# Attention scores of a hybrid decoder layer as half-array products, with keys and transposes laid out for it

## The chip, the cores and the metric

One core of one Trainium2 chip runs the whole layer as one program. The metric is the device time of one execution in microseconds (us). Before the change the median of three runs is 2406.98 us (2406.73 to 2409.63).

## The reference, cut to what matters

One decoder layer over 2048 tokens of width 1024, all in 32-bit floats. After a modulated RMS norm, one input projection feeds two parallel groups of heads: sliding-window attention (8 query heads of 64, 2 key/value heads, window 128, a learned sink per head) and a state-space scan. Both go through one output projection; then come a second norm, a SwiGLU feed-forward part and a last norm. The change touches the attention alone:

```python
def sliding_window_attention(q, k, v, sinks):
    ...
    kb, vb = band(k), band(v)          # the token block before and the block itself
    scores = jnp.einsum('bnqhgd,bnkhd->bnhgqk', qb, kb).astype(jnp.float32)
    scores = scores * (1.0 / math.sqrt(HEAD_DIM))
    ...
    mask = (diff >= 0) & (diff < WINDOW) & (kpos[:, None, :] >= 0)
    scores = jnp.where(mask[None, :, None, None], scores, -jnp.inf)
    ...
    m = jnp.maximum(jnp.max(scores, axis=-1, keepdims=True), sink)
    p = jnp.exp(scores - m)
    denom = jnp.sum(p, axis=-1, keepdims=True) + jnp.exp(sink - m)
    probs = (p / denom).astype(v.dtype)
    out = jnp.einsum('bnhgqk,bnkhd->bnqhgd', probs, vb)
```

The sum over d, the 64 elements of a head, is the product that the change rebuilds: q has heads g = 0 to 3 for each key group h = 0 and 1.

## The kernel before

The tokens are cut into 4 blocks of 512 (b = 0 to 3), each into 4 token tiles of 128 (t). Every operand of a large product is split into a high part that TensorE takes as it is and a low part that holds the rest (`split`, `halves`: a copy on ACT, a subtraction on DVE or POOL), and a product is three matmuls: high by high, high by low, low by high (`mm3`, lines 272 to 275). A matmul names its stationary operand first (the weights that PEld loads), then the moving one; its name in the profile is out<-moving,stationary.

The program runs a main stream of dense products on TensorE (queries, keys and values, convolution inputs, gates, output projection, then the feed-forward part as `quads` and `down`) and puts *side steps* between its chunks: `attentions(b)` and `ssds(b)` are generators, each `yield` ends one side step, and `beside` takes on average 1.1 (MIX), 0.5 or 0.64 side steps after each chunk of the main stream. `both` takes a step of the one and a step of the other in turn. A chunk is mostly twelve dense matmuls.

TensorE's instructions follow the order in which the code issues them up to the end of `gated(3)` (a manual schedule); later ones, and those of DVE, ACT, POOL and the DMA queue, are placed by a scheduler that works with estimated times. Each engine then runs its own instructions in order.

TensorE's results lie in eight banks of 128 partitions by 512 floats: four for the dense products (d), and one each for am, at, sm and st. A bank with one buffer can't be written anew before its last reader is done. Attention has am and at, the scan has sm and st.

For each token tile, `attentions` goes through these steps:
- It turns the keys (one 128x128 transpose into am, line 549) and the queries (four into at, line 557). Partitions 0 to 63 of the turned keys belong to key group 0, partitions 64 to 127 to group 1. `k_ring` holds them for two tiles, high and low, with each group in a 128-row operand whose other 64 rows are zero (lines 551 to 554), so that one matmul over 128 rows gives both groups side by side: 128 queries by 256 columns. Queries are split by lines 560 and 561.
- For j = 0 to 3 (query head j of both groups), `scores` makes two times three matmuls of 256 columns into am (one `mm3` for the tile before, one for the tile itself), and two reductions on DVE (line 609) add the mask, store the scores and keep the maximum.
- After j = 3, `probabilities` does eight exponentials with their sums and eight scalings on ACT (lines 620 and 626).
- The tile before is held back by one round: its `transposed` (four 128x128 transposes into at, line 632, with a copy on ACT and a subtraction on DVE, lines 635 and 636) runs ahead of each `scores`, and after every second one `values` makes twelve matmuls with v_ring into am, which line 646 copies out.

Of the kernel before, what the change touches and what calls it, by code (L numbers as in the profile page):

```python
# [42 lines left out]
def hymba_layer(ctx, tc, xT, crow, pos, wada, wadk, vecs, rows, wq, wkv, wz, wx, wo, wgu, wd4, wd2, outT):  # L43
# [18 lines left out]
    def bank(tag, bufs):  # L62
        return pp.tile([P, T], F32, name=tag, tag=tag, bufs=bufs)
# [36 lines left out]
    def const(shape, name, dt=F32, pool=sb):  # L100
        return pool.tile(shape, dt, name=name, tag=name, bufs=1)
# [27 lines left out]
    amask = const([P, 2 * P], "amask")  # L129
    nc.gpsimd.memset(amask, 0.0)  # L130
    nc.gpsimd.affine_select(out=amask[:, 0:P], in_=amask[:, 0:P], pattern=[[1, P]], compare_op=ALU.is_ge,
                            fill=NEG, base=-1, channel_multiplier=-1)
# [338 lines left out]
    k_ring = const([P, 2, 2, 2, P], "k_ring", F32R)  # L471
    v_ring = const([P, 4 * 192 + 64], "v_ring", F32R)
    nc.gpsimd.memset(k_ring.bitcast(F32), 0.0)
# [40 lines left out]
    def attentions(b, m):  # L514
        late = []

        def values_of(sms, slots, t):
            got = {}

            def turn(j):  # L520
                if j % 2 == 0:
                    got["pT"] = [m.m4().rearrange("p h t -> p (h t)").rearrange("p (b j k) -> p b j k", b=4, j=2)
                                 for _ in range(2)]
                transposed(sms[j], got["pT"], len(slots), j % 2)

# [7 lines left out]
            return turn, sums  # L533
# [10 lines left out]
        for t in range(NT):  # L544
            gt, (q, kv) = b * NT + t, nxt
            slot = gt % 2
            slots = [slot] if gt == 0 else [1 - slot, slot]
            ps = bank("am", 1)
            nc.tensor.transpose(ps[:, 0:P], kv[:, 0:P], ident)
            for r in range(2):  # L550
                rs = slice(r * 64, (r + 1) * 64)
                nc.scalar.copy(k_ring[rs, 0, slot, r, :], ps[rs, 0:P])
                nc.vector.tensor_tensor(k_ring[rs, 1, slot, r, :], ps[rs, 0:P],
                                        k_ring[rs, 0, slot, r, :].bitcast(F32), ALU.subtract)
# [41 lines left out]
    def scores(m, st, qhi, qlo, slots, j):  # L596
        mx = st[:, 0, :]
        ns = len(slots)
        mask = amask[:, (2 - ns) * P:].rearrange("p (s k) -> p s k", k=P)
        sc = bank("am", 1)[:, :2 * P * ns]  # L600
        js = slice(j * P, (j + 1) * P)
        for i, slot in enumerate(slots):
            mm3(sc[:, 2 * P * i:2 * P * (i + 1)], qhi[:, js], qlo[:, js],
                *(k_ring[:, h, slot].rearrange("p r k -> p (r k)") for h in range(2)), True, True)
        sc = sc.rearrange("p (s r k) -> p s r k", r=2, k=P)
        sm = m.m2().rearrange("p (r s k) -> p r s k", r=2, k=P)
        for r in range(2):
            i = 2 * j + r
            nc.vector.tensor_tensor_reduce(sm[:, r, 0:ns, :], sc[:, :, r, :], mask, 1.0, sinks[:, i:i + 1],
                                           ALU.add, ALU.max, mx[:, i:i + 1])  # L610
        return sm
# [784 lines left out]
```

## Time and profile before

| what | us |
|---|---|
| median of the three runs | 2406.98 |
| the profiled execution | 2408.73 |
| its span, first to last instruction | 2407.0 |
| PE busy (TensorE, matmul) | 2267.8 |
| DVE busy | 1445.4 |
| POOL busy | 1230.1 |
| ACT busy | 966.2 |

The mean clock granted to TensorE was 0.971. PE is TensorE's matmul stream, PEld its weight loads, which run beside it; DVE, ACT and POOL are VectorE, ScalarE and GpSimd. A record's start is real; the end of a matmul is modelled, so the time that one holds the stream is read from start to start. In a row of the timeline the first number is the start, the second the duration, and in brackets stands how long the engine had been idle before and what ended it. A row such as "PE am L273 <- DVE k_ring L553: 9.6, 6, 3.8" says that PE, at line 273 into am, waited for DVE's line 553 for 9.6 us in total, 6 times, 3.8 at the longest.

### The profile page before, as it was taken

To read this page: it belongs to the slowest core of one execution; us is meant where nothing else is said; L and a number is where in the kernel's file an instruction comes from. 1 tells how busy PE (TensorE), PEld (TensorE's weight loads), DVE (VectorE), ACT (ScalarE), POOL (GpSimd) and SP (SyncE) were. 2 spreads that over 40 slices of the span, in tenths; PEclk is the share of its full clock that TensorE was granted. 3 is DMA by queue.
4 is the path that set the end of the run, shared out by engine and by line. 5 is a ranking of instruction groups with operands and counts; after the bars stand their busy time and mean duration, and the time that the engine had idled before them with its cause. 6 is when DMAs were issued, how large, how long until landed. Compare 5 with 4: busy or idle time off the path is not lost.

```text
span 2407.0 us, 33175 instructions
## 1 busy us (share of the span) xinstructions
PE 2267.8 (94%) x11304; PEld 1887.6 (78%) x11304; DVE 1445.4 (60%) x2543; ACT 966.2 (40%) x2011; POOL 1230.1 (51%) x1227
## 2 busy tenths in 40 slices
PE   6896999999999899999999999989999999999998
PEld 4786889798879688887887788766788888878787
DVE  6877875664455865566664363499555444544544
ACT  2464552654345545533333232244333333333332
POOL 0866433453113755578785232446766666643441
PEclk9897999999999899999999999999999999999998
DMA  6798977777875422232334665574422222263441
GB/s 242 271 367 286 309 245 252 235 249 241 281 243 173 135 85 66 84 110 89 96 101 153 230 221 165 189 264 154 142 88 79 80 83 79 79 227 101 142 160 53
DMA packets 249065, 412.22 MB, mean 171 GB/s; under 512 B 22464, under 2 KB 68544, under 8 KB 248896
## 3 DMA queue, kind: packets, MB, share of 16 engines
q1 hardware_dynamic: 247744, 409.05, 51.5%
q8 instruction: 89, 1.46, 0.3%
q10 hardware_dynamic: 1152, 1.05, 0.1%
q14 instruction: 80, 0.66, 0.1%
HBM read 315.58 MB, written 94.44 MB: 170 GB/s over the span
## 4 chain that ended last, share of the span: by engine, by line
PE 67%; DVE 12%; DMA 7%; POOL 5%; issue 5%; ACT 3%; SPq 1%; DVEq 0%; POOLq 0%; ACTq 0%
PE d L273 9%; PE d L275 9%; PE d L274 9%; PE d L881 7%; PE d L880 7%; PE d L882 7%; DMA t<-in_xT_dram 2%; PE am L273 1%; PE am L274 1%; PE am L275 1%; PE am L880 1%; DMA t<-act 1%; PE am L882 1%; PE am L881 1%; DMA t<-mid 1%
## 5 line engine op out<-in xcount | busy, mean ns | idle before, releaser
L880 PE MATMUL d<-b,w 128*128 128x512 f32 x924 | 366.2, 400 | 12.0 <-ACT b L841 9.2
L881 PE MATMUL d<-b,w 128*128 128x512 f32 x924 | 368.4, 399 | 0.9 <-POOL b L842 0.9
L882 PE MATMUL d<-b,w 128*128 128x512 f32 x924 | 366.8, 398 | 0.7 <-DVE w L812 0.7
L811 ACT ACTIVATE w<-raw 128x512 fp32r<-128x512 f32 x316 | 197.5, 629 | 415.9 <-PE d L275 212.6
L273 PE MATMUL d<-a,w 128*128 128x512 f32 (+1 forms) x720 | 281.1, 398 | 22.8 <-ACT a L961 12.2
L275 PE MATMUL d<-a,w 128*128 128x512 f32 (+1 forms) x720 | 283.2, 393 | 0.0
L274 PE MATMUL d<-a,w 128*128 128x512 f32 (+1 forms) x720 | 281.9, 392 | 0.1
L812 DVE TENSOR_TENSOR w<-raw,w 128x512 fp32r<-128x512 f32 x228 | 213.1, 937 | 72.8 <-ACT w L811 72.1
L812 POOL TENSOR_TENSOR w<-raw,w 128x512 fp32r<-128x512 f32 x88 | 119.9, 1363 | 247.3 <-ACT w L811 228.4
L972 DVE SCALAR_TENSOR_TENSOR x<-d,mod,x 128x512 f32<-128x512 f32 (+1 forms) x182 | 130.7, 724 | 162.5 <-PE d L275 159.8
L880 PEld LDWEIGHTS d<-b,w 128*128 128x128 f32 x924 | 174.7, 189 | 53.5 <-ACT b L841 11.8
L273 PE MATMUL d<-w,hl 128*128 128x256 f32 (+1 forms) x608 | 181.4, 299 | 27.4 <-ACT hl L324 12.7
L881 PEld LDWEIGHTS d<-b,w 128*128 128x128 f32 x924 | 175.2, 190 | 39.9 <-POOL b L842 1.9
L882 PEld LDWEIGHTS d<-b,w 128*128 128x128 f32 x924 | 174.5, 189 | 39.8 <-DVE w L812 1.4
L812 POOL TENSOR_TENSOR w<-s,w 128x512 fp32r<-128x512 f32 x132 | 188.2, 1428 | 30.6 <-ACT w L811 29.6
L811 ACT ACTIVATE w<-s 128x512 fp32r<-128x512 f32 x176 | 110.8, 633 | 200.3 <-PE d L882 156.7
L273 PEld LDWEIGHTS d<-a,w 128*128 128x128 f32 x720 | 137.0, 191 | 60.6 <-ACT a L961 15.1
L275 PE MATMUL d<-w,hl 128*128 128x256 f32 (+1 forms) x608 | 177.7, 292 | 2.4 <-DVE hl L325 2.4
L274 PE MATMUL d<-w,hl 128*128 128x256 f32 (+1 forms) x608 | 177.2, 292 | 0.0
L274 PEld LDWEIGHTS d<-a,w 128*128 128x128 f32 x720 | 137.1, 190 | 31.6 <-DVE a L806 0.9
L896 POOL TENSOR_TENSOR s<-raw,s 128x512 f32<-128x512 f32 x44 | 59.3, 1349 | 199.1 <-DVE w L812 124.4
L275 PEld LDWEIGHTS d<-a,w 128*128 128x128 f32 x720 | 136.7, 190 | 30.8 <-issue 0.2
(356 smaller groups left out, 5486.9 us busy)
## 6 DMA issues: line engine op xcount, KB each, us to landing
raw<-in_wgu_dram SPq DMA_DIRECT2D x176, 256.0 KB, 2.7
raw<-in_wd_dram SPq DMA_DIRECT2D x176, 256.0 KB, 2.7
w<-w_x SPq DMA_DIRECT2D x48, 512.0 KB, 5.3
w<-w_o SPq DMA_DIRECT2D x48, 512.0 KB, 4.7
act<-t SPq DMA_DIRECT2D x88, 256.0 KB, 2.1
t<-act SPq DMA_DIRECT2D x88, 256.0 KB, 4.4
t<-in_xT_dram SPq DMA_DIRECT2D x80, 256.0 KB, 4.4
aw<-in_wada_dram SPq DMA_DIRECT2D x64, 256.0 KB, 4.5
```

The source lines that it names most:

```text
L273: nc.tensor.matmul(out, ahi, bhi, start=first, stop=False)
L274: nc.tensor.matmul(out, ahi, blo, start=False, stop=False)
L275: mm3.last = nc.tensor.matmul(out, alo, bhi, start=False, stop=last)
L811: nc.scalar.activation(hi, x, AF.Copy)
L812: eng.tensor_tensor(lo, x, hi.bitcast(F32), ALU.subtract)
L880: nc.tensor.matmul(out, ahi, bhi, start=first and k == 0, stop=False, skip_group_check=True)
L881: nc.tensor.matmul(out, ahi, blo, start=False, stop=False, skip_group_check=True)
L882: mm3.last = nc.tensor.matmul(out, alo, bhi, start=False, stop=k == 3, skip_group_check=True)
L896: nc.gpsimd.tensor_tensor(s4, a12, s2, ALU.subtract)
L972: nc.vector.scalar_tensor_tensor(x, ps, gate2[:, c:c + 1], x, ALU.mult, ALU.add)
```

## The change

- The keys are kept without zeros: `k_ring` is half as large, and one cast and one subtraction of 128 partitions replace two of each over 64.
- The scores of two query heads (`pair_of`) are made in one go: for each, three products by two halves r. A half takes partitions 64r to 64r + 63 of queries and keys, 64 rows of the array, and 256 columns (both tiles at once); group 0 goes to bank am and group 1 to bank at, alternating. That is twelve matmuls, then four reductions.
- The ring's slots stay in place, so the mask has a third part, and is taken rotated where the tile itself lies in slot 0.
- Transposes come in pairs: four into am, four into at, and `values` is the step after them. Scores of a pair, transposes of a pair and values of a half are side steps of their own. `probabilities` comes in the step of the second pair of scores, ahead of the transposes of the second pair.

```diff
-    amask = const([P, 2 * P], "amask")
+    amask = const([P, 3 * P], "amask")
...
-    k_ring = const([P, 2, 2, 2, P], "k_ring", F32R)
+    k_ring = const([P, 2, 2, P], "k_ring", F32R)
     v_ring = const([P, 4 * 192 + 64], "v_ring", F32R)
-    nc.gpsimd.memset(k_ring.bitcast(F32), 0.0)
...
         def values_of(sms, slots, t):
             got = {}
 
-            def turn(j):
-                if j % 2 == 0:
-                    got["pT"] = [m.m4().rearrange("p h t -> p (h t)").rearrange("p (b j k) -> p b j k", b=4, j=2)
-                                 for _ in range(2)]
-                transposed(sms[j], got["pT"], len(slots), j % 2)
-
-            def sums(half):
+            def turn(half):
+                pT = [m.m4().rearrange("p h t -> p (h t)").rearrange("p (b j k) -> p b j k", b=4, j=2)
+                      for _ in range(2)]
+                for j in range(2):
+                    transposed(sms[2 * half + j], pT, len(slots), j)
+                yield
                 if half == 0:
                     got["out"] = m.m2()
-                values(got["out"], got["pT"], slots, half)
+                values(got["out"], pT, slots, half)
                 if half:
                     nc.sync.dma_start(spill[b][0:4, :, t * P:(t + 1) * P].rearrange("c p t -> p c t"),
                                       got["out"].rearrange("p (c t) -> p c t", c=4))
-            return turn, sums
+                yield
+            return turn
 
         def load(t):
             q, kv = m.m2(), m.m1()
...
         for t in range(NT):
             gt, (q, kv) = b * NT + t, nxt
             slot = gt % 2
-            slots = [slot] if gt == 0 else [1 - slot, slot]
+            slots = [0] if gt == 0 else [0, 1]
+            mask = amask[:, P:2 * P] if gt == 0 else amask[:, (1 - slot) * P:(3 - slot) * P]
             ps = bank("am", 1)
             nc.tensor.transpose(ps[:, 0:P], kv[:, 0:P], ident)
-            for r in range(2):
-                rs = slice(r * 64, (r + 1) * 64)
-                nc.scalar.copy(k_ring[rs, 0, slot, r, :], ps[rs, 0:P])
-                nc.vector.tensor_tensor(k_ring[rs, 1, slot, r, :], ps[rs, 0:P],
-                                        k_ring[rs, 0, slot, r, :].bitcast(F32), ALU.subtract)
+            nc.scalar.copy(k_ring[:, 0, slot, :], ps[:, 0:P])
+            nc.vector.tensor_tensor(k_ring[:, 1, slot, :], ps[:, 0:P], k_ring[:, 0, slot, :].bitcast(F32), ALU.subtract)
             ps = bank("at", 1)
             for j in range(4):
                 nc.tensor.transpose(ps[:, j * P:(j + 1) * P], q[:, j * P:(j + 1) * P], ident)
...
             st = small([P, 4, 8], "ast", 1)
             yield
             sms = []
-            for j in range(4):
+            for pair_of in range(2):
+                sms.extend(scores(m, st, qhi, qlo, slots, mask, pair_of))
+                if pair_of:
+                    probabilities(st, sms, slots)
+                    if t + 1 < NT:
+                        nxt = load(t + 1)
+                yield
                 if held:
-                    held[0](j)
-                sms.append(scores(m, st, qhi, qlo, slots, j))
-                if j == 3:
-                    probabilities(st, sms, slots)
-                if j == 2 and t + 1 < NT:
-                    nxt = load(t + 1)
-                yield
-                if held and j % 2:
-                    held[1](j // 2)
-                    if j == 1:
-                        yield
+                    yield from held(pair_of)
             load_values(kv, slot)
-            if held:
-                yield
             held = values_of(sms, slots, t)
-        for j in range(4):
-            held[0](j)
-            yield
-            if j % 2:
-                held[1](j // 2)
-                yield
+        for half in range(2):
+            yield from held(half)
 
     def load_values(kv, slot):
         v = kv[:, P:2 * P].rearrange("p (r d) -> p r d", d=64)
...
-    def scores(m, st, qhi, qlo, slots, j):
+    def scores(m, st, qhi, qlo, slots, mask, pair_of):
+
         mx = st[:, 0, :]
         ns = len(slots)
-        mask = amask[:, (2 - ns) * P:].rearrange("p (s k) -> p s k", k=P)
-        sc = bank("am", 1)[:, :2 * P * ns]
-        js = slice(j * P, (j + 1) * P)
-        for i, slot in enumerate(slots):
-            mm3(sc[:, 2 * P * i:2 * P * (i + 1)], qhi[:, js], qlo[:, js],
-                *(k_ring[:, h, slot].rearrange("p r k -> p (r k)") for h in range(2)), True, True)
-        sc = sc.rearrange("p (s r k) -> p s r k", r=2, k=P)
-        sm = m.m2().rearrange("p (r s k) -> p r s k", r=2, k=P)
-        for r in range(2):
-            i = 2 * j + r
-            nc.vector.tensor_tensor_reduce(sm[:, r, 0:ns, :], sc[:, :, r, :], mask, 1.0, sinks[:, i:i + 1],
-                                           ALU.add, ALU.max, mx[:, i:i + 1])
-        return sm
+        mask = mask.rearrange("p (s k) -> p s k", k=P)
+        banks = [bank("am", 1), bank("at", 1)]
+        for e in range(2):
+            js = slice((2 * pair_of + e) * P, (2 * pair_of + e + 1) * P)
+            for n, (q, h) in enumerate(((qhi, 0), (qhi, 1), (qlo, 0))):
+                for r in range(2):
+                    rs = slice(r * 64, (r + 1) * 64)
+                    nc.tensor.matmul(banks[r][:, 2 * e * P:(2 * e + ns) * P], q[rs, js],
+                                     k_ring[rs, h, 0:ns, :].rearrange("p s k -> p (s k)"), start=e == 0 and n == 0,
+                                     stop=e == 1 and n == 2, skip_group_check=True)
+        sms = []
+        for e in range(2):
+            sm = m.m2().rearrange("p (r s k) -> p r s k", r=2, k=P)
+            for r in range(2):
+                i = 2 * (2 * pair_of + e) + r
+                sc = banks[r][:, 2 * e * P:(2 * e + ns) * P].rearrange("p (s k) -> p s k", k=P)
+                nc.vector.tensor_tensor_reduce(sm[:, r, 0:ns, :], sc, mask, 1.0, sinks[:, i:i + 1],
+                                               ALU.add, ALU.max, mx[:, i:i + 1])
+            sms.append(sm)
+        return sms
...
     def transposed(sm, pT, ns, at):
-        ps = bank("at", 1)
+        ps = bank(("am", "at")[at], 1)
         for s in range(ns):
             for r in range(2):
                 nc.tensor.transpose(ps[:, (2 * s + r) * P:(2 * s + r + 1) * P], sm[:, r, s, :], ident)
```

In what order the engines now run this is shown at three places; a row is line, operation, out<-in and size, x4 four alike in a row.

PE at a group of scores. Before, in block 0 (t = 2), after four transposes:

```order
L275 MATMUL d<-w,hl_1485 128x264
L632 MATMUL at<-ident,m_1765 128x128 x4
L273 MATMUL am<-k_ring,m_2378 128x256
L274 MATMUL am<-k_ring,m_2378 128x256
L275 MATMUL am<-k_ring,m_2378 128x256
L273 MATMUL am<-k_ring,m_2378 128x256
L274 MATMUL am<-k_ring,m_2378 128x256
L275 MATMUL am<-k_ring,m_2378 128x256
L273 MATMUL d<-w,hl_1492 128x264
```

After, in the same tile:

```order
L275 MATMUL d<-w,hl_1526 128x256
L276 MATMUL d<-w,hl_1526 128x256
L595 MATMUL am<-k_ring,m_2198 128x256
L595 MATMUL at<-k_ring,m_2198 128x256
L595 MATMUL am<-k_ring,m_2198 128x256
L595 MATMUL at<-k_ring,m_2198 128x256
```

The alternation of am and at goes on to twelve products. Before, six products of the full array follow the transposes; now twelve of half the array lie between dense products, and the transposes are elsewhere.

PE at the end of block 1, where the last tile's probabilities are turned and multiplied by the values. Before:

```order
L275 MATMUL d<-w,hl_5759 128x256
L632 MATMUL at<-ident,m_6633 128x128 x4
L273 MATMUL d<-w,hl_5766 128x256
L274 MATMUL d<-w,hl_5766 128x256
L275 MATMUL d<-w,hl_5766 128x256
```

After:

```order
L276 MATMUL d<-hl_5766,w 128x512
L628 MATMUL am<-ident,m_6371 128x128 x4
L628 MATMUL at<-ident,m_6374 128x128 x4
L274 MATMUL am<-m_6709,v_ring 128x256
L275 MATMUL am<-m_6710,v_ring 128x256
L276 MATMUL am<-m_6709,v_ring 128x256
```

Before, dense products follow the transposes, and the value products come 24 dense matmuls later; now they stand right behind the pair of transposes.

ACT at the probabilities of a tile in block 1. Before:

```order
L635 ACTIVATE m_5213<-at 128x4x128
L444 COPY cin<-d 128x512
L447 ACTIVATE s<-cin,vec 128x512
L448 ACTIVATE s<-cin,vec 128x512
L635 ACTIVATE m_5213<-at 128x4x128
L452 ACTIVATE s<-s 128x512
L620 ACTIVATE m_5029,ast<-m_5029,ast 128x256 x2
L620 ACTIVATE m_5108,ast<-m_5108,ast 128x256 x2
L620 ACTIVATE m_5229,ast<-m_5229,ast 128x256 x2
L620 ACTIVATE m_5300,ast<-m_5300,ast 128x256 x2
L621 ACTIVATE ast<-ast 128x8
```

After:

```order
L616 ACTIVATE m_5361,ast<-m_5361,ast 128x256 x2
L616 ACTIVATE m_5364,ast<-m_5364,ast 128x256 x2
L616 ACTIVATE m_5684,ast<-m_5684,ast 128x256 x2
L616 ACTIVATE m_5687,ast<-m_5687,ast 128x256 x2
L617 ACTIVATE ast<-ast 128x8
L252 ACTIVATE hl_5756<-t 128x512
L631 ACTIVATE m_5802<-am 128x4x128
L631 ACTIVATE m_5802<-at 128x4x128
```

Before, the copies of the held tile's transposes (line 635) stand ahead of the exponentials (line 620); now the copies of the second pair (line 631) stand behind them (line 616).

More of the change, by code (lines that the diff above doesn't have):

```diff
@@ L128, in hymba_layer @@
     later = later_r.bitcast(F32)
-    amask = const([P, 2 * P], "amask")
+    amask = const([P, 3 * P], "amask")
     nc.gpsimd.memset(amask, 0.0)
-    nc.gpsimd.affine_select(out=amask[:, 0:P], in_=amask[:, 0:P], pattern=[[1, P]], compare_op=ALU.is_ge,
-                            fill=NEG, base=-1, channel_multiplier=-1)
+    for before in (amask[:, 0:P], amask[:, 2 * P:3 * P]):
+        nc.gpsimd.affine_select(out=before, in_=before, pattern=[[1, P]], compare_op=ALU.is_ge, fill=NEG, base=-1,
+                                channel_multiplier=-1)
     nc.gpsimd.affine_select(out=amask[:, P:2 * P], in_=amask[:, P:2 * P], pattern=[[-1, P]],
```

## The prediction

> **What bounds the kernel now.** I read the page first, then stretches of the span, then the score products themselves. On the page I look at TensorE's busy time (PE) and at the chain that ended last.
>
> ```profile
> span 2407.0 us, 33175 instructions
> PE 2267.8 (94%) x11304; PEld 1887.6 (78%) x11304; DVE 1445.4 (60%) x2543; ACT 966.2 (40%) x2011; POOL 1230.1 (51%) x1227
> PE 67%; DVE 12%; DMA 7%; POOL 5%; issue 5%; ACT 3%; SPq 1%; DVEq 0%; POOLq 0%; ACTq 0%
> ```
>
> TensorE is busy 94% of the span and is two thirds of the chain; no other engine is above 60%. What shortens its stream therefore shortens the run, where it is not waiting for something else. The stretches show where that is. Columns: length, busy time of PE, PEld, DVE, ACT, POOL, then granted clock, DMA share, GB/s; the last row, of the score products alone, has PE's busy time and count before clock and DMA.
>
> ```profile
> 436.00:456.00 20.00, 14.84 (x66) 11.96 (x65) 14.65 (x28) 14.17 (x29) 9.31 (x22) 0.83 0.61 205
> 456.00:560.00 104.00, 101.87 (x636) 89.92 (x635) 66.52 (x143) 60.56 (x151) 52.23 (x69) 1.00 0.77 258
> 120.00:200.00 80.00, 5.03 (x30) 0.91 1.03 367
> ```
>
> From 456 to 560 us PE is busy 98% at full clock: a microsecond less there is a microsecond less of run. From 120 to 200 us the DMA engines are full (share 1.03), and shorter products gain nothing; 30 of the score products lie there. From 436 to 456 us a wait has cost clock too (0.83).
>
> The score products, from the view of the instructions that touch k_ring (nanoseconds: shortest, median, longest), and one group of six with its neighbours in the timeline:
>
> ```profile
> L273 PEld LDWEIGHTS am<-k_ring,m x124: 186/189/337, 127.5 to 999.4; 128*128 128x128 f32 x124
> L273 PE MATMUL am<-k_ring,m x124: 274/282/583, 127.5 to 999.5; 128*128 128x256 f32 x124
> L552 ACT CAST k_ring<-am x32: 238/260/262, 123.4 to 969.8; 64x128 fp32r<-64x128 f32 x32
> L553 DVE TENSOR_TENSOR k_ring<-am,k_ring x32: 271/288/296, 124.2 to 970.1; 64x128 fp32r<-64x128 f32 x32
> ```
>
> ```profile
> 453.19 0.60 PE L632 MATMUL at<-ident,m 128*128 128x128 f32 x4
> 453.54 0.36 PE L273 MATMUL am<-k_ring,m 128*128 128x256 f32 x1
> 453.74 0.28 PE L274 MATMUL am<-k_ring,m 128*128 128x256 f32 x1
> ...
> 454.34 0.40 PE L273 MATMUL d<-hl,w 128*128 128x512 f32 x1
> 454.57 0.40 PE L274 MATMUL d<-hl,w 128*128 128x512 f32 x1
> ```
>
> Five steps lie between 453.74 and 454.34: a score product holds the stream for 0.12 us, though its record says 0.28 (starts are real, ends modelled). The first of the six takes 0.20: leaving the transposes costs 0.08 us. A dense product of 512 columns takes 0.23, so a chunk of twelve, the usual distance between two side steps, is 2.8 us. The product of three is written as lines 273 to 275, so x124 stands for 3 x 124 = 372 products: 372 x 0.12 = 44.6 us of stream.
>
> **The change, part by part.**
>
> *Half-array products.* By the order of PE there are 384 of them, in 192 pairs of the two halves. Each works on 64 rows, each with its own weight load of 128 columns. Nothing in this trace multiplies on half the rows. The nearest rows are those that use one row (line 178) or one column (line 171):
>
> ```profile
> L178 PEld LDWEIGHTS am<-ones,t x16: 181/187/328, 31.8 to 55.9; 1*128 1x128 f32 x16
> 47.20 0.28 PE L275 MATMUL st<-w,hl 128*128 128x256 f32 x1
> 47.41 7.03 PE L171 MATMUL am<-m,vec 128*1 128x512 f32 x16
> ...
> 55.10 1.05 PE L178 MATMUL am<-ones,t 1*128 1x2 f32 x8 [0.67 <-ACT t L176]
> ...
> 56.08 0.39 PE L273 MATMUL d<-w,hl 128*128 128x256 f32 x1
> 56.31 0.28 PE L274 MATMUL d<-w,hl 128*128 128x256 f32 x1
> 56.42 0.28 PE L275 MATMUL d<-w,hl 128*128 128x256 f32 x1
> ```
>
> A load of one row takes 187 ns, like the 189 of 128 rows, and eight products of 2 columns take 56.08 - 55.10 = 0.98 us, 0.12 each: on this path the load alone sets a pace of 0.12, and fewer rows make it no cheaper. So the change gains only if the two halves' loads and products both run side by side. Upper end of the gain: 192 pairs at 0.12 are 23.0 us, 21.6 less than now. Lower end: nothing runs side by side, 384 x 0.12 = 46.1, 1.5 more. I take the upper: halves that share no row, no partition and no bank have nothing in these rows to queue for, and the trace already has a load run under a product (a load of 189 ns at a pace of 0.12). Of it the 8% in the DMA-bound stretch (30 of 372) falls away: **-19.9 us**.
>
> The Trainium skill, "TensorEngine Tiling (Array Packing)", section "Tiling Modes", says that different tiles can load weights and multiply in parallel, and that changing the mode drains TensorE; no run here shows the first yet. By the first the sum would be the one taken.
>
> *Boundaries.* In the new order 38 runs of half products begin and 38 end (32 groups, six split by the scheduler): 76 changes of shape. Going into line 171 the step is 0.21 instead of 0.12, coming out of line 178 it is 0.23 against 0.11: 0.1 us each, **+7.6 us**. Lower end 0 (the array need not empty; a boundary can't gain). Upper end: the array empties (0.28) and then loads (0.19) before the next product, 0.35 more than the pace of 0.12: +26.6 us. I take 0.1, the two real changes of shape.
>
> *Transposes in pairs.* PE leaves transposes for other work 88 times now and 54 times after; at 0.08 us that is **-2.7 us**.
>
> *Keys in one piece.* ACT and DVE have 16 casts and 16 subtractions less (16 x 0.26 and 16 x 0.288 us), hidden on engines that are not the bound. But the split in two shows in a wait. PE's longest waits at attention, in total, times and longest, and the worst of them in the timeline of its three engines:
>
> ```profile
> PE am L273 <- DVE k_ring L553: 9.6, 6, 3.8
> PE at L632 <- DVE m L561: 8.4, 4, 4.3
> PE am L273 <- DVE ast L609: 2.9, 1, 2.9
> PE at L632 <- ACT m L626: 2.1, 2, 1.5
> ```
>
> ```profile
> 437.97 0.24 ACT L552 CAST k_ring<-am 64x128 fp32r<-64x128 f32 x1
> 438.24 0.28 DVE L553 TENSOR_TENSOR k_ring<-am,k_ring 64x128 fp32r<-64x128 f32 x1 [1.59 <-ACT k_ring L552]
> 441.60 0.26 ACT L552 CAST k_ring<-am 64x128 fp32r<-64x128 f32 x1
> 443.67 0.29 DVE L553 TENSOR_TENSOR k_ring<-am,k_ring 64x128 fp32r<-64x128 f32 x1
> 444.02 0.58 PE L273 MATMUL am<-k_ring,m 128*128 128x256 f32 x1 [3.82 <-DVE k_ring L553]
> ```
>
> The first half of the keys is ready at 438.5; the second waits in both queues behind other work until 444.0. In one piece it would be ready with the first. Of the 9.6 us I count 6 as gone, and 2 of the 3.4 us that the clock of 0.83 loses in those 20 us: **-8 us**. Where this stall goes, the queries' lower half (line 561, finished at 439.4 here) is late next.
>
> *New waits.* Each side step now takes both banks, am and at, so scores wait for the last copies and transposes for the last reductions. What each reader takes:
>
> ```profile
> L609 DVE CUSTOM_DVE_ANT_0 m<-am,amask,row x128: 339/478/489, 128.2 to 1000.4; 128x256 f32<-128x256 f32 x120, 128x128 f32<-128x128 f32 x8
> L609 DVE DVE_READ_ACCUMULATOR2_ANT ast<- x128: 74/82/90, 128.5 to 1000.9; 128x1 f32 x128
> L635 ACT ACTIVATE m<-at x64: 366/597/614, 161.6 to 1034.6; 128x512 fp32r<-128x512 f32 x60, 128x256 fp32r<-128x256 f32 x4
> L636 DVE TENSOR_TENSOR m<-at,m x64: 410/685/694, 162.9 to 1036.7; 128x512 fp32r<-128x512 f32 x60, 128x256 fp32r<-128x256 f32 x4
> L620 ACT ACTIVATE m<-m,ast x128: 385/494/512, 150.0 to 1005.2; 128x256 f32<-128x256 f32 x120, 128x128 f32<-128x128 f32 x8
> L620 ACT ACTIVATION_READ_ACCUMULATOR m<-m,ast x128: 184/187/192, 150.3 to 1005.6; 128x1 f32 x128
> ```
>
> After scores: 4 x (0.478 + 0.082) = 2.2 us of DVE before the transposes may write. After a pair of transposes: 2 x 0.597 on ACT and 0.685 on DVE behind them, 1.9 us before the value products. Both fit into one chunk of 2.8 us, when the queues are empty. By the order there are seven places with one chunk between a pair of transposes and its values, and one with none (the end of block 1); the others have two. I count 1.9 us for the one and 0.6 (one ACT instruction ahead in the queue) for each of the seven: **+6 us**. On ACT the copies of the second pair now also stand behind the eight exponentials, 8 x (0.494 + 0.187) = 5.4 us. Before they stood ahead. The values that wait for them come two steps after, 11 us with attention and state-space steps in turn, which covers it: nothing, but up to 5 us a block step if the cover goes.
>
> The rest: the clearing of k_ring on POOL and the wider mask lie in the first microseconds, 120 us before their first use: nothing. The DMAs are the same in number and size. Four side steps fewer a block only end the side work earlier.
>
> Sum: -19.9 + 7.6 - 2.7 - 8 + 6 = -17.0 us. The profiled execution took 2408.7 us (span 2407.0 and 1.7 around it), so 2391.7. The median of the runs is 1.75 us below the profiled one: **2390 us**, -0.7%. Its own range is 2379 to 2400, from 0 to 0.25 us a boundary and waits of 7 us more or less.
>
> **The rivals.**
>
> *The halves don't overlap* (the change does not do what it says). For it: a load costs the same for one row as for 128, the pace of 0.12 equals the load's, and no row shows two loads at once. Against: the two halves share nothing. Then +1.5 + 7.6 - 2.7 - 8 + 6 = +4.4, 2411 us (+0.2%), with 2404 to 2418 by boundaries and waits. The same comes out if a half can't take its next weights while it multiplies: load 0.12 and product 0.12 in turn, two halves in opposite phase, one product per 0.12. The Trainium skill, "TensorE: Matmul & The Clock Gate", section "Part 3: Packing small matmuls", states this as a rule (a load overlaps products in flight only on other row groups), but the trace disagrees for the full array, where loads of 189 ns keep a pace of 0.12 on the same rows.
>
> *Slower: the hand-off of the two banks.* There are 7 side steps for each of 16 token tiles, 112 hand-offs. Now the waits above are 23.0 us, 0.2 us a hand-off. Scores had am and transposes had at, so the two could be in flight together; now each step waits for the readers of the last. If the average grows by 0.28 us (half a reduction) that is +31 us: 2421. It ends slower from +22 us on, 0.2 us a hand-off. [...] Against: the next step is a chunk or two away nearly everywhere.
>
> *The boundary costs 0.35 us*, and the halves overlap: +19 on the forecast, 2409, no change. Against: the two changes of shape in the trace cost a third of it.
>
> **How the numbers follow.** Forecast 0.52, no overlap 0.28, hand-off 0.10, boundary 0.10. Within 0.2% (4.8 us) is about what a measurement of this kernel can't tell from no change: 2402.2 to 2411.8. Faster 0.50 (the forecast but for 0.02). Same 0.29: 0.18 of no overlap, 0.07 of the boundary, 0.02 of the hand-off and 0.02 of the forecast. Slower 0.21: 0.10, 0.08 and 0.03 of no overlap, hand-off and boundary. The range from 2379 to 2415 leaves out the hand-off and the upper part of no overlap, some 0.2.
>
> **What would show it.** In the changed profile: starts of line 595 in pairs, a pair each 0.12 us (right) or one product each 0.12 (no overlap). The first dense product after a group 0.1 later than its pace, or 0.35. PE's waits for k_ring below 4 us in total. Waits of the value products on line 632 and of the transposes on the score reductions: 6 us in total, or 30 and more. I am wrong if the pair takes 0.24, or if these waits outgrow the 17 us.

## The result and the profile after

The changed kernel takes 2435.7 us (median of four runs, 2431.0 to 2440.0); the kernel before, run beside it, takes 2408.3. The ratio is 1.0103, with a 95% interval of 1.0082 to 1.0124: 25 us slower, where 2390 was forecast. The profiled execution took 2440.0 us, with a span of 2438.3.

The head of its page, and the shares of the chain that ended last:

```profile
span 2438.3 us, 33202 instructions
PE 2277.9 (93%) x11316; PEld 1883.7 (77%) x11316; DVE 1449.6 (59%) x2527; ACT 960.4 (39%) x1995; POOL 1236.6 (51%) x1227
PE 70%; DVE 12%; DMA 5%; issue 5%; POOL 4%; ACT 3%; SPq 0%; DVEq 0%; POOLq 0%; ACTq 0%
```

No other engine has become the bound. Next, the instructions that touch k_ring (nanoseconds: shortest, median, longest) and one group of score products with its neighbours in PE's timeline:

```profile
L595 PEld LDWEIGHTS am<-k_ring,m x192: 182/185/189, 127.8 to 955.5; 64*128 64x128 f32 x192
L595 PE MATMUL am<-k_ring,m x192: 270/278/386, 127.8 to 955.6; 64*128 64x256 f32 x180, 64*128 64x128 f32 x12
```

```profile
445.32 0.40 PE L275 MATMUL d<-hl,w 128*128 128x512 f32 x1
445.57 0.40 PE L276 MATMUL d<-hl,w 128*128 128x512 f32 x1
445.89 0.38 PE L595 MATMUL am<-k_ring,m 64*128 64x256 f32 x1
445.90 0.38 PE L595 MATMUL at<-k_ring,m 64*128 64x256 f32 x1
446.12 0.28 PE L595 MATMUL am<-k_ring,m 64*128 64x256 f32 x1
446.12 0.28 PE L595 MATMUL at<-k_ring,m 64*128 64x256 f32 x1
446.23 0.28 PE L595 MATMUL am<-k_ring,m 64*128 64x256 f32 x1
446.24 0.28 PE L595 MATMUL at<-k_ring,m 64*128 64x256 f32 x1
...
446.60 0.28 PE L595 MATMUL at<-k_ring,m 64*128 64x256 f32 x1
446.80 0.50 PE L274 MATMUL d<-hl,w 128*128 128x512 f32 x1
447.14 0.40 PE L275 MATMUL d<-hl,w 128*128 128x512 f32 x1
447.38 0.40 PE L276 MATMUL d<-hl,w 128*128 128x512 f32 x1
```

The two halves start within 0.01 us of each other and a pair holds the stream for 0.12 us: they overlap fully, loads of 185 ns included. The price stands at the edges. Four steps are longer than their pace: the step into the group (445.57 to 445.89, 0.32 instead of 0.23), the first pair (0.23 instead of 0.12), the step out (446.60 to 446.80, 0.20 instead of 0.12) and the first dense product (0.34 instead of 0.23). That is 0.39 us a group, 0.2 for each change of shape.

PE's waits, first those of the attention that the prediction spoke of and one that it did not, then the two that grew most elsewhere (in total, times, longest):

```profile
PE am L275 <- DVE m L632: 8.0, 6, 2.1
PE am L274 <- DVE m L632: 5.5, 4, 2.2
PE am L628 <- DVE ast L604: 3.4, 2, 1.9
PE am L274 <- ACT m L631: 1.8, 2, 1.3
PE at L595 <- ACT k_ring L551: 0.7, 1, 0.7
PE at L555 <- DMA m<-q: 5.3, 2, 4.1
```

```profile
PE d L274 <- ACT a L957: 25.9, 6, 10.3
PE st L671 <- ACT m L751: 12.8, 2, 7.2
```

The wait for the keys has gone from 9.6 us to 0.7. The first four lines above (values wait for the transposes' copies and subtractions, transposes for the reductions) come to 18.7 us; in their place the prediction's list had 13.4. Neither list is complete: the queries' transposes now wait 5.3 us for their load. All of PE's waits in front of the attention's products and transposes, added up, are 30.2 us after 24.5. In front of the value products they grew from 2.9 to 19.5. More is lost outside the attention: the down products (d, L274) wait 25.9 us for the casts of their inputs, line 957 (before: 12.2, 5 times, 3.0 at the longest), and the scan's transposes (st, L671) 12.8 us for line 751 (before: 2.6). The stretch from 1340 to 1760 us, where the output projection and the down products share the stream, first before, then after (length, PE, PEld, DVE, ACT, POOL, clock, DMA share, GB/s):

```profile
1340.00:1760.00 420.00, 401.94 (x1710) 319.20 (x1709) 258.79 (x368) 143.03 (x241) 205.28 (x148) 0.99 0.57 189
```

```profile
1340.00:1760.00 420.00, 385.00 (x1594) 305.52 (x1593) 240.79 (x350) 133.23 (x222) 181.53 (x129) 0.96 0.57 181
```

PE is busy 17 us less there, at a clock of 0.96 instead of 0.99. The worst wait of that stretch, in the timeline of SP's DMA queue and of PE:

```profile
1562.48 0.33 SPq L779 DMA_DIRECT2D mid<-t  x1
1562.86 1.90 SPq L955 DMA_DIRECT2D t<-act  x4
```

```profile
1568.96 1.65 PE L274 MATMUL d<-a,w 128*128 128x512 f32 x3 [10.33 <-ACT a L957]
```

SP's queue issues its instructions in order. The loads of the next inputs of the down products (line 955) follow right behind the store of an output-projection chunk (line 779); they are issued at 1562.86, and the products that need them start at 1568.96, after 10.33 us of standing still. In the order of PE, 168 of the output projection's 384 products now stand ahead of the first down product; before, there were 120.

### The profile page after: what moved, and what is told of

Same layout as the page of the kernel before. It is cut to its first block, busy times and chain, and to the rows that moved or that the text cites. A ratio compares the mean times of both kernels' runs of the same rounds, so it can differ in the third digit from the quotient of the medians.

```text
span 2438.3 us, 33202 instructions
## 1 busy us (share of the span) xinstructions
PE 2277.9 (93%) x11316; PEld 1883.7 (77%) x11316; DVE 1449.6 (59%) x2527; ACT 960.4 (39%) x1995; POOL 1236.6 (51%) x1227
## 4 chain that ended last, share of the span: by engine, by line
PE 70%; DVE 12%; DMA 5%; issue 5%; POOL 4%; ACT 3%; SPq 0%; DVEq 0%; POOLq 0%; ACTq 0%
PE d L274 10%; PE d L275 10%; PE d L276 10%; PE d L876 7%; PE d L878 7%; PE d L877 7%; DVE aw L194 1%; DMA aw<-in_wada_dram 1%; PE am L876 1%; PE am L878 1%; PE am L877 1%; PE am L275 1%; DVE t L827 1%; PE am L276 1%; PE am L274 1%
## 5 line engine op out<-in xcount | busy, mean ns | idle before, releaser
L274 PE MATMUL d<-a,w 128*128 128x512 f32 (+1 forms) x720 | 285.4, 404 | 29.9 <-ACT a L957 25.9
L275 PE MATMUL d<-a,w 128*128 128x512 f32 (+1 forms) x720 | 284.7, 396 | 3.9 <-DVE a L802 3.8
L276 PE MATMUL d<-a,w 128*128 128x512 f32 (+1 forms) x720 | 285.3, 396 | 0.0
L274 PE MATMUL d<-w,hl 128*128 128x256 f32 (+1 forms) x608 | 181.5, 299 | 18.1 <-DVE s L375 7.5
L274 PEld LDWEIGHTS d<-a,w 128*128 128x128 f32 x720 | 139.9, 195 | 66.1 <-ACT a L957 28.5
L275 PEld LDWEIGHTS d<-a,w 128*128 128x128 f32 x720 | 138.9, 193 | 36.8 <-DVE a L802 4.6
L276 PEld LDWEIGHTS d<-a,w 128*128 128x128 f32 x720 | 138.4, 192 | 31.1 <-issue 0.2
L284 POOL TENSOR_TENSOR acc<-acc,t 128x512 f32<-128x512 f32 x70 | 95.4, 1365 | 125.9 <-ACT t L283 110.0
```

Source lines behind the costliest of these rows:

```text
L274: nc.tensor.matmul(out, ahi, bhi, start=first, stop=False)
L275: nc.tensor.matmul(out, ahi, blo, start=False, stop=False)
L276: mm3.last = nc.tensor.matmul(out, alo, bhi, start=False, stop=last)
L284: eng.tensor_tensor(acc, acc, sq, ALU.add)
```

## The experiments

Each was timed beside the kernel before. To compare the kernels, a ratio is turned into microseconds of 2408; by that measure the changed kernel stands at +24.8 (+19.7 to +29.9).

| kernel | median, us | ratio to before (95%) | us of 2408 |
|---|---|---|---|
| e1 after, 4 empty side steps a block | 2395.3 | 0.9936 (0.9921 to 0.9951) | -15.4 |
| e2 the same in block 3 alone | 2413.5 | 1.0015 (1.0003 to 1.0027) | +3.6 |
| e6 after, 4 empty steps behind the last scan | 2412.2 | 1.0014 (1.0000 to 1.0028) | +3.4 |
| e4 before, 4 side steps a block fewer | 2438.8 | 1.0119 (1.0101 to 1.0137) | +28.7 |
| e8 before, more empty side steps | 2427.6 | 1.0085 (1.0062 to 1.0108) | +20.5 |
| e3 after, products over all rows | 2431.3 | 1.0089 (1.0071 to 1.0108) | +21.4 |
| e5 e1, products over all rows | 2396.8 | 0.9949 (0.9931 to 0.9968) | -12.3 |
| e9 e1, every third product over all rows | 2419.6 | 1.0033 (1.0017 to 1.0049) | +7.9 |
| e11 e1, halves one after the other | 2392.9 | 0.9915 (0.9896 to 0.9934) | -20.5 |
| e7 e1, keys split in two again | 2399.8 | 0.9963 (0.9949 to 0.9977) | -8.9 |
| e10 e1, transposes in one bank | 2495.1 | 1.0349 (1.0332 to 1.0365) | +84.0 |

### Is it the count of side steps?

Theory A: the loss comes from four side steps fewer a block, which shifts the scan and the output projection against the main stream. Theory B: it comes from the attention itself. The first kernel gives the steps back as empty ones.

```diff
                 if held:
                     yield from held(pair_of)
+                elif True:
+                    yield
...
         for half in range(2):
-            yield from held(half)
+            for i, _ in enumerate(held(half)):
+                yield
+                if i == 0 and True:
+                    yield
```

> The changed kernel with empty side steps put back, so that each attention block has as many as before (two more in the first tile, two more at the end). Theory A (the loss is a shift of the output projection of blocks 2 and 3 against the quads and the down products, because attention has fewer side steps): what counts is not the number of steps but where the projection ends up. By the order of PE 168 of its 384 products still stand ahead of the first down product, as in the changed kernel, where before had 120; so 2425 to 2440 us, and PE's idle time between the start and the end of down(0) stays near 20 us. Theory B (the loss is in attention itself: hand-offs of the two banks and changes of shape): the empty steps give the hand-offs more room, 2415 to 2430 us.

It takes 2395.3 us, below both ranges, 40 us less than the changed kernel. Theory A's range was worked out for 168 products of the output projection ahead of the first down product; in the order as run there are 120, as before, so that its condition does not hold. The number speaks for the side steps as the cause, but not yet against theory B, since the empty steps at the end of each block stand between transposes and values. Against theory B speaks that PE's waits in front of the attention's instructions hardly move: 27.6 us here, 30.2 in the changed kernel. The stretch of the down products is whole again, and the scan's wait is back at 2.6 us:

```profile
1340.00:1760.00 420.00, 405.20 (x1718) 323.26 (x1719) 259.78 (x371) 145.96 (x245) 209.73 (x150) 0.99 0.55 183
```

```profile
PE st L676 <- ACT m L756: 2.6, 1, 2.6
```

The second kernel has the same empty steps in the last block alone (`elif b == 3`, and `if i == 0 and b == 3`).

> The changed kernel with the same empty side steps in block 3 alone. By the order of PE 120 products of the output projection stand ahead of the first down product, as before the change. Theory A: the loss behind the attention goes, 2405 to 2418 us. Theory B: 2430 to 2440 us, since attention of blocks 0 to 2 is the changed kernel's.

2413.5 us, with 120 products ahead: within theory A's range; the last block's four steps are worth 21 of the 40 us, those of the other blocks the remaining 19.

The sixth puts four empty steps behind the last scan, so that no step of the attention is moved against a step of the scan:

```diff
-    sides.extend([attentions(3, common), ssds(2, stepping[2], common), ssds(3, stepping[3], common)])
+    sides.extend([attentions(3, common), ssds(2, stepping[2], common), ssds(3, stepping[3], common),
+                  (None for _ in range(4))])
```

> The changed kernel with four empty side steps between the end of the last scan block and the start of the output projection of block 2; attention and scan are untouched. By the order of PE 120 products of the output projection then stand ahead of the first down product (168 in the changed kernel, 120 before). Theory A (the place of the output projection is what costs behind the attention): like e2_pad_last, 2410 to 2420 us, and no wait of 10 us at the start of down(1). Theory H (the empty steps of e2_pad_last helped inside attention of block 3, not behind it): 2430 to 2440 us.

2412.2 us, the same as e2. Four empty steps that touch no engine, at the very end of the side work, gain 21 us: this part of the loss comes from where the side work ends, and with it from the output projection's place. The down products wait 13.8 us here, 3.9 at the longest, where the changed kernel has 25.9 and 10.3. The scan's wait, which belongs to the blocks before (at 389 and 455 us in the changed kernel), is still there in both (12.3 and 12.2 us), and so is the wait for the queries' load (4.7 in both).

The fourth takes the same number of steps away from the kernel *before*, with nothing else changed:

```diff
-                yield
+                if held or j % 2:
+                    yield
...
         for j in range(4):
             held[0](j)
-            yield
             if j % 2:
+                yield
                 held[1](j // 2)
                 yield
```

> The kernel before with four side steps fewer in each attention block and nothing else changed (full-array products, zero-padded keys). By the order of PE 168 products of the output projection then stand ahead of the first down product, as in the changed kernel. Theory A: the loss comes without the change, 2420 to 2435 us. Theory B: 2404 to 2413 us.

2438.8 us: beyond theory A's range, and as slow as the change itself. Its trace shows the same picture without any half-array product: the stretch, the scan's wait, SP's queue and the wait of PE behind it. Not all of its 29 us is the place of the side work, though: without the steps between them, two groups of transposes at the end of each block follow each other in the bank at, and two of scores in the first tile in am, and PE's waits in front of the attention's instructions are 35.3 us, where the kernel before has 24.5.

```profile
1340.00:1760.00 420.00, 382.60 (x1599) 303.24 (x1598) 239.19 (x350) 133.63 (x222) 176.95 (x129) 0.97 0.56 181
```

```profile
PE st L676 <- ACT m L756: 9.5, 2, 7.2
```

```profile
1559.96 0.33 SPq L784 DMA_DIRECT2D mid<-t  x1
1560.34 1.90 SPq L960 DMA_DIRECT2D t<-act  x4
```

```profile
1565.56 2.07 PE L273 MATMUL d<-a,w 128*128 128x512 f32 x4 [9.38 <-ACT a L962]
```

The eighth asks whether more steps are better still, on the kernel before, with four empty ones more in each block (two in the first tile, two at the end):

```diff
                 if held and j % 2:
                     held[1](j // 2)
                     if j == 1:
                         yield
+                elif j % 2:
+                    yield
...
                 held[1](j // 2)
                 yield
+                yield
```

> The kernel before with two to four more empty side steps in each attention block, the mirror of e4_before_fewer. By the order of PE 72 products of the output projection stand ahead of the first down product (120 before). Theory A1 (each shift of the side steps against the main stream changes the waits, in either direction): off by more than 5 us from 2411 us, up or down. Theory A2 (only too few steps cost, since the scan and the output projection are then without a neighbour): 2406 to 2414 us.

2427.6 us, theory A1, with 72 products of the output projection ahead: too many cost as well. Its loss lies in the same stretch, where PE is busy 387 us; the down products wait 24.2 us for their inputs, 11.0 at the longest:

```profile
1340.00:1760.00 420.00, 386.71 (x1629) 307.43 (x1628) 241.67 (x352) 134.11 (x225) 189.13 (x135) 0.97 0.57 183
```

So it isn't "later is better" but a place that fits. Of the three that were tried in the kernel before, 120 products ahead cost least; 72 cost 20 us more, and 168, with the attention's waits above, 29.

### What are the half-array products worth?

The third kernel takes the half rows back inside the changed kernel:

```diff
-                    rs = slice(r * 64, (r + 1) * 64)
-                    nc.tensor.matmul(banks[r][:, 2 * e * P:(2 * e + ns) * P], q[rs, js],
-                                     k_ring[rs, h, 0:ns, :].rearrange("p s k -> p (s k)"), start=e == 0 and n == 0,
+                    nc.tensor.matmul(banks[r][:, 2 * e * P:(2 * e + ns) * P], q[:, js],
+                                     k_ring[:, h, 0:ns, :].rearrange("p s k -> p (s k)"), start=e == 0 and n == 0,
```

> The changed kernel with its twelve score products over all 128 rows instead of 64 (each score then sums both key groups, so the attention's values are others; the work, the banks and the steps are the same). It prices the half-array form alone. If the halves run side by side and a change of shape costs 0.1 to 0.2 us, the score stream grows by 22 us and 76 changes of shape fall away (8 to 15 us): 2440 to 2452 us. If the form were what costs the 27 us (theory C), it comes out below the changed kernel, at 2410 to 2425 us.

2431.3 us, not slower but 4 us faster by the medians, within the intervals: neither range was met, and there is no verdict, since both kernels carry the shifted side work. The fifth makes the same edit in e1, where that is gone:

> The changed kernel with its side steps put back as in e1_pad_all (2395 us), and its twelve score products over all 128 rows instead of 64 (each score then sums both key groups; the values are others, the work is the same). It prices the half-array form where the side steps stand as before. Theory F (my terms: halves side by side save 22 us of stream, the changes of shape cost 0.1 to 0.2 us each, 8 to 15 us): 2402 to 2409 us. Theory G (e3_full_rows, where full rows were 4 us faster than halves: the form brings nothing): 2388 to 2396 us.

2396.8 us, 1.4 slower than e1 (3.1 by the ratios): 0.8 above theory G's range, five below theory F's. A full group of e5 in PE's timeline takes 1.42 us (642.89 to 644.31), and its neighbours keep their pace:

```profile
642.65 0.39 PE L276 MATMUL d<-hl,w 128*128 128x512 f32 x1
642.89 0.28 PE L600 MATMUL am<-k_ring,m 128*128 128x256 f32 x1
643.00 0.28 PE L600 MATMUL at<-k_ring,m 128*128 128x256 f32 x1
...
644.31 0.40 PE L274 MATMUL d<-m,w 128*128 128x512 f32 x1
644.55 0.39 PE L275 MATMUL d<-m,w 128*128 128x512 f32 x1
```

With halves the same group takes 0.91 (445.89 to 446.80 above), and 0.2 more goes into the dense products on both sides. So a full group gains 1.42 - 0.91 - 0.20 = 0.31 us; the 27 groups of e1 that stay whole make 8.4. The scheduler splits the other five. Three of them become six products of one half and, after a chunk of dense products, six of the other, here in the changed kernel:

```profile
857.15 0.97 PE L595 MATMUL at<-k_ring,m 64*128 64x256 f32 x6
858.05 0.50 PE L876 MATMUL d<-b,w 128*128 128x512 f32 x1
```

These six have no partner to overlap with: they take 0.90 us, as long as twelve in pairs, and full rows take 0.72 for the same six in e5. With its edges such a group loses 0.8 us, and the other two lose 0.5 together. That leaves some 5.6 us, of which 3 arrive in the time (the two intervals, 4 us each way, allow both).

The ninth measures the change of shape by itself, with four more of them inside each group:

```diff
-                    rs = slice(r * 64, (r + 1) * 64)
+                    rs = slice(0, P) if n == 1 else slice(r * 64, (r + 1) * 64)
```

> The padded kernel (2395.3), in which the middle third of each group's score products (high queries by low keys) takes all 128 rows, so that each head's pairs read half, full, half: the sum of that third runs over both key groups, so the scores aren't the reference's, and the side steps and the order are as before. A group keeps its changes at both ends and gets four more changes of shape inside, 38 groups: 152 more. Its stream grows by two pairs a group of 0.12 us each at most: +8 (with all rows full it grew by 23.6). Theory J (a change of the number of rows costs about 0.2 us itself, whichever way): 2395.3 + 8 + 30 = 2433, range 2422 to 2445. Theory K (what is lost at the ends of a group comes from the banks, from other work or from the first load, and not from the change): 2395 + 8 = 2403, range 2396 to 2408. At the predicted 0.1 it would be 2418.

2419.6 us: 23 to 24 us over e1, between the ranges of J and K and, by the time alone, what 0.1 us a change would give. The trace decides. One group:

```profile
467.58 0.40 PE L276 MATMUL d<-hl,w 128*128 128x512 f32 x1
467.90 0.38 PE L600 MATMUL am<-k_ring,m 64*128 64x256 f32 x1
467.91 0.38 PE L600 MATMUL at<-k_ring,m 64*128 64x256 f32 x1
468.22 0.39 PE L600 MATMUL am<-k_ring,m 128*128 128x256 f32 x1
468.44 0.28 PE L600 MATMUL at<-k_ring,m 128*128 128x256 f32 x1
468.65 0.38 PE L600 MATMUL am<-k_ring,m 64*128 64x256 f32 x1
...
469.83 0.50 PE L274 MATMUL d<-hl,w 128*128 128x512 f32 x1
```

It takes 1.93 us (467.90 to 469.83) instead of 0.91. The two pairs that now run one product at a time add 2 x 0.12; the rest, 0.78, is four changes: 0.2 us each, whichever way. That is theory J's price. In the whole trace PE is busy 33 us longer than in e1 (2294.0 after 2261.1), and 24 of these arrive in the time, since its idle time fell from 132.8 to 123.6 us (span less busy time): what waited for something else waits less when PE is late.

The eleventh asks whether the overlap needs the halves to alternate:

```diff
-            for n, (q, h) in enumerate(((qhi, 0), (qhi, 1), (qlo, 0))):
-                for r in range(2):
+            for r in range(2):
+                for n, (q, h) in enumerate(((qhi, 0), (qhi, 1), (qlo, 0))):
```

> The padded kernel (2395.3) with the loops over the halves and over the three products exchanged: all three products on rows 0 to 63, then all three on rows 64 to 127, for each query head. Same products, same result, same changes of shape at a group's ends. Theory L (two half-array products overlap only where neighbours in the order are on different rows): only the product at each seam overlaps, 3 of 12 in a group, so a group of 24 products takes some 21 x 0.12 instead of 12 x 0.12: 38 groups x 9 x 0.12 (less in the first tile) = +17 to +22 for pace alone: 2408 to 2418. Theory M (the rows' queues run free of each other over several products): 2393 to 2399.

2392.9 us: theory M, 0.1 below its range. By the ratio it is 20 us faster than the kernel before (16 to 25) and 45 faster than the change, the fastest version of all, though against e1 the intervals overlap. A full group takes 0.91 us here too (the next one, 459.28 to 460.19), though the instructions come as three into am, three into at, three into am, three into at. A group in which the third product has to wait for the lower half of the queries shows the order:

```profile
437.83 0.47 PE L600 MATMUL am<-k_ring,m 64*128 64x256 f32 x2
439.53 0.38 PE L600 MATMUL am<-k_ring,m 64*128 64x256 f32 x1 [1.23 <-DVE m L559]
439.53 0.38 PE L600 MATMUL at<-k_ring,m 64*128 64x256 f32 x1
439.75 0.28 PE L600 MATMUL am<-k_ring,m 64*128 64x256 f32 x1
439.76 0.28 PE L600 MATMUL at<-k_ring,m 64*128 64x256 f32 x1
```

The products into at stand behind the third into am and wait with it. Then the fourth product into am starts at 439.75 together with the second into at, ahead of the third into at, which stands before it in the code.

### The keys and the transposes

The seventh splits the cast and the subtraction of the keys into two halves of 64 partitions again, in e1:

```diff
-            nc.scalar.copy(k_ring[:, 0, slot, :], ps[:, 0:P])
-            nc.vector.tensor_tensor(k_ring[:, 1, slot, :], ps[:, 0:P], k_ring[:, 0, slot, :].bitcast(F32), ALU.subtract)
+            for r in range(2):
+                rs = slice(r * 64, (r + 1) * 64)
+                nc.scalar.copy(k_ring[rs, 0, slot, :], ps[rs, 0:P])
+                nc.vector.tensor_tensor(k_ring[rs, 1, slot, :], ps[rs, 0:P], k_ring[rs, 0, slot, :].bitcast(F32),
+                                        ALU.subtract)
```

> e1_pad_all with the keys cast and subtracted in two halves of 64 partitions again, as before the change. Theory F (my term of 8 us for the keys in one piece): 2400 to 2406 us, with waits of PE for k_ring of 5 us or more in total. Theory I (with the steps as they are now the second half has time enough): 2393 to 2399 us.

2399.8 us, 4.4 slower than e1 by the medians and 6.5 by the ratios, between the two ranges. PE's waits for the keys return, 10.6 us against 1.8 in e1:

```profile
PE am L603 <- DVE k_ring L554: 10.6, 5, 4.7
```

The tenth puts both groups of transposes of a pair into the bank at:

```diff
-        ps = bank(("am", "at")[at], 1)
+        ps = bank("at", 1)
```

> The padded kernel (2395.3) with both groups of transposes of a pair in the bank at, as each was before, instead of one in am and one in at; order and side steps unchanged. The second group has to wait until the first has been copied out and subtracted (0.72 + 0.55 us or so, and the hand-overs), 32 pairs. Theory N (the second bank is what makes the pair worth its 7 us): 30 waits of about 1.5 us = +45, 2430 to 2450, since nothing stands between the two. Theory O (the waits are covered, because the scheduler or the weight loads run ahead): 2393 to 2402.

2495.1 us: theory N's direction at twice its price, far above its range. One line of the waits carries 71 us of it, and the mean granted clock of the run is 0.957 (e1: 0.971):

```profile
PE at L633 <- DVE m L637: 70.8, 21, 8.4
```

This isn't what the pairs gain over the kernel before, where a step of scores stood between two groups of transposes. It prices a hand-over with nothing between: 3.4 us on average, and up to 8.4 where ACT has a tile's exponentials and scalings in its queue ahead of the copy.

## Why the prediction was wrong

- **The step that failed** is "Four side steps fewer a block only end the side work earlier", priced at nothing. The four steps cost 40 us (after against e1). The sentence named no work that hides this and did not ask what moves when the side work ends earlier. Where it ends is worth 21 us by itself (e6): the output projection's stores then stand in SP's in-order queue ahead of the down products' loads, and PE waits up to 10.3 us for them. The kernel before with four steps fewer a block is 29 us slower (e4); PE's waits in front of the attention are 11 us more there, so that not all of it is the place. The order was at hand, and the count of 168 against 120 could be read from it. No rival covered it.
- **What stays open**: the steps of the first three blocks are worth the other 19 us. The scan's wait is 10 us of them in the traces and the wait for the queries' load 5; no run isolates either, nor why the scan waits longer. Of the 44 us between the two profiled executions 28 are idle time of PE and 17 longer busy time, at a mean granted clock of 0.965 against 0.971.
- **Boundaries** were mis-sized. They were put at 0.1 us, +7.6 us in all; they measure 0.2 us, some +15. The prediction read one longer step at each change; there are two, of 0.1 each. The Trainium skill, "TensorEngine Tiling (Array Packing)", section "Tiling Modes", has the drain at a change of mode; e9 gives its size here, 0.2 us each way.
- **Half-array products** overlap as forecast: a pair each 0.12 us, and the 0.28 chance of no overlap is refuted. With the boundaries the term was to be -12.3 us; the rows make it -5.6, the time -3.1 (e5 against e1; e5 has 384 full products, the kernel before 372). The term counted all 192 pairs as pairs, but in three groups the scheduler puts the halves apart, and 36 products have no partner.
- **Keys in one piece**: the mechanism is right, the wait is gone (0.7 us). The term of -8 measures -4.4 to -6.5.
- **New waits** were counted at +6, and this term was far too small: in front of the value products PE waits 19.5 us, 2.9 before. That the listed lines rise by only 5.3 us (18.7 against 13.4) is luck: 8.4 us in front of the transposes went, which the sum had kept. By the prediction's own sign, waits that outgrow 17 us, it was wrong here. Yet this is not where the loss lies: e1 has 20.3 us in front of the value products and takes 2395.3.
- **Transposes in pairs** (-2.7) and these waits were to be +3.3 together. What is left of e1's -15.4 after halves (-3.1) and keys (-6.5) is -6, with intervals of some 6 us. No run separates the two; that is open.
- **Hand-off of two banks**, the rival at 2421, comes closest to the time by accident: it puts the loss into the attention, where PE's waits grew by 5.7 us, and e1, with the same banks, runs at 2395.

With the side steps restored (e1), the change gains 15.4 us where the sum had 17.0. That they agree so well is luck: the terms have errors of both signs.

## What to carry to other kernels

Where side work is fed into a main stream step by step, the number of its steps is a schedule: an edit that makes fewer of them moves everything behind, and the first comparison is the same kernel with empty steps in their place. Empty steps behind all side work then tell what its end alone is worth. Price a change of array shape by all four steps that it touches, here 0.4 us a visit, so that a group of half products has to save more than that, and look in the order of PE whether each half still has its partner beside it. When an edit removes waits, list all of those that go, not only the longest.

## What the runs showed of the hardware

Products on different halves of the array's rows overlap in full: a pair takes 0.12 us, as one product of full rows does and as one half does without a partner. They run free of each other over several instructions: in e11 a group written three by three takes the same 0.91 us as one written in turn, with starts that leave the order of the code. The Trainium skill, "TensorE: Matmul & The Clock Gate", section "Part 3: Packing small matmuls", calls products strictly first in, first out; the starts at 439.75 us differ. A change between half and full rows costs 0.2 us each way, about half of it in the step itself and half in the step after.
